# Three settings of the value phase: which sums keep a bank of their own, which bank comes first, and where the gather steps stand

## The chip, the cores and the metric

The kernel runs on one core of a Trainium2 chip. The metric is the device time of one execution in microseconds (us); lower is better. A core has TensorE (matmuls, called PE in the profile, its weight loads PEld), VectorE (DVE), ScalarE (ACT), GpSimd (POOL, which here issues the gathers of rows) and SyncE (SP, which issues the other loads). They run side by side, each through its own queue in order, and wait for one another by semaphores. Matmuls write into PSUM, which has eight banks of 128 x 512 f32 here.

## What is computed

One decoder layer: a mixer (recurrence and short convolution), then PEER, a retrieval of single-neuron experts, and a final norm. The change lies in PEER, cut here to what matters:

```python
q = (xb @ w_query).reshape(T, PEER_HEADS, 2, PEER_HALF)
s = jnp.einsum('thpk,hpnk->thpn', q, sub_keys)
...                                   # top 16 of each half, top 16 of their pairs: idx, gate
u = expert_u[idx]                     # 8 heads x 16 experts of 16384, 1024 wide
v = expert_v[idx]
act = jax.nn.gelu(jnp.einsum('td,thkd->thk', xb, u), approximate=False)
return jnp.einsum('thk,thkd->td', gate * act, v)
```

## The kernel before

The 1024 tokens are treated in two ways. For the last 672 (TD) the product with the experts is dense: all 16384 experts are taken in 128 blocks of 128 (NK = 128), every activation is computed, and a gate matrix that is zero for the experts not chosen is multiplied in. For the first 352 tokens the chosen rows of u and v are gathered from memory one expert a step, and VectorE does the sums ("gather steps"). These steps are a generator, `background()`, which the code of the dense part advances as it goes, so that both run side by side.

Every f32 operand of a matmul is split in a high part (ACT, L115) and a rest (VectorE, L116), and a product takes three matmuls: high x high, high x rest, rest x high.

The last stage (L1345 to the end) loops over the 128 blocks. For a block it does

- `u_steps`: the product of h2 with the block of u. The 672 tokens are two halves of 384 and 288 columns (SPL); each half has 24 matmuls (L1163) into one of two banks named `pa`, and ACT takes its GELU (L1168) into a tile `Wl`. Forty of the blocks (EARLIES, every third from 1 to 118) were computed in earlier stages and are loaded instead (L1450, `ged`);
- `w_step`: VectorE multiplies the gates in (L1384), then the split into `Wh` and `Wl`;
- `v_load`: the block of v is loaded and split into `vh` and `vl`.

After every third block comes a value phase (`v_phase`) of the three blocks before: 16 sums, one for each of the two halves (j = 0: 384 columns, j = 1: 288) and eight chunks of 128 outputs (c), in the order (0, 0) to (0, 7), (1, 0) to (1, 7). Each is nine matmuls (L1403). Four of the sums (FIXED) have a PSUM bank `pacc` of their own that keeps accumulating through all phases and is read once at the end. The twelve others take banks in turn from `new_pv`, alternately one of the two `pa` that the u blocks use too and one of two named `pv`; VectorE adds each into a sum in SBUF (`acc`, L1419), which frees the bank. Two and two and four banks are all eight.

A gather step is a row fetch issued on POOL (L1084, 128 rows of 4 KB) into one of five row buffers (four named `grow`, and `more` for every fifth), and one VectorE instruction on 128 x 1024: L1102 with a row of u, L1094 with a row of v. `advance(cost)` adds to an amount due and emits steps until the amount spent reaches it. In this stage `along(columns)` calls it, after every k of `u_steps` with the columns of three matmuls (L1455 to L1457), and after every sum of a value phase but the last phase's. So the steps are spread by the columns of TensorE's work (L1372 to L1377).

A scheduler then sets the order of each engine's queue from this program; the order below is its output.

Of the kernel before, what the change touches and what calls it, by code (L numbers as in the profile page):

```python
# [30 lines left out]
NK = 128  # L31
# [19 lines left out]
EARLY = 40  # L51
# [2 lines left out]
ROWS = 4  # L54
TB = 8
NE = 3.6
NF = 2.1 * TG / 64
MID = 1
WL = 3
# [2 lines left out]
WB = 2  # L62
WJ = 0
PAIRS = [(0, 2), (2, 4)]
FIXED = [(0, 1), (0, 5), (1, 1), (1, 5)]
RB = 0.15
RD = 0.0
DG = 2
# [31 lines left out]
def build(tc, A, out, dbg=None):  # L100
# [17 lines left out]
    def raw_tile(pl, shape, name, lb):  # L118

        return pl.tile(shape, F32R, name=name + "l", bufs=lb).bitcast(F32)  # L120
# [21 lines left out]
    with root:  # L142
# [29 lines left out]
        def advance(cost):  # L172
            if bg["back"] is None:
                return
            bg["due"] += cost
            while bg["spent"] < bg["due"]:
                bg["spent"] += next(bg["back"], 1e9)
# [826 lines left out]
        def norm_store(pl, o, w, parts, fw, r, sq):  # L1004

            sf = pl.tile([P, 4], F32, name="sf", bufs=3)[:w]
            for j in range(2):
                C.activation(sq[:w], parts[j], AF.Square, accum_out=sf[:, j:j + 1])
            V.scalar_tensor_tensor(sf[:, 0:1], sf[:, 0:1], DM * EPS, sf[:, 1:2], op0=OP.add, op1=OP.add)
            rsqrt(sf[:, 2:3], sf[:, 0:1], sf[:, 3:4], 5)  # L1010
            for j in range(2):
                sl = slice(j * 512, j * 512 + 512)
                V.scalar_tensor_tensor(r[:w, sl], parts[j], sf[:, 2:3], fw[:w, sl], op0=OP.mult, op1=OP.mult)
            SY.dma_start(out[o:o + w], r[:w])
# [140 lines left out]
        def u_steps(b, ge):  # L1155

            uh, ul = stationary("uT", b)
            for o, n in SPL:
                pa = psU.tile([P, 512], F32, name="pa", bufs=2)
                i = 0  # L1160
                for k in range(KC):
                    for l, r in ((uh, "h"), (uh, "l"), (ul, "h")):
                        T.matmul(pa[:, :n], l[:, k], h2[k, r][:, o:o + n], start=(i == 0), stop=(i == 3 * KC - 1))  # L1163
                        i += 1
                    if k == MID:
                        ahead()
                    if k == KC - 1:
                        C.activation(ge[:, o:o + n], pa[:, :n], AF.Gelu)  # L1168
                    yield 3.0 * n
# [10 lines left out]
        def u_early(blocks, rate):  # L1180

            left = blocks * 3.0 * KC * TD
            while left > 0:
                c = next(early, None)
                if c is None:
                    return False
                left -= c
                advance(c / 2400.0 * RATES[rate])
            return True
# [33 lines left out]
        def early_along(steps_):  # L1223
            for c in steps_:
                fill[0] += c * NE / 26.0
                if fill[0] - fill[1] > 0.25:
# [16 lines left out]
        for g in range(FULL, NG):  # L1243
            o, w = GG[g]
            r = slice(P - REST + o, P - REST + o + w)
            n = steps[g]
# [42 lines left out]
        def gates(t):  # L1289
# [3 lines left out]
            for q4 in range(w // TG):  # L1293
# [17 lines left out]
                for qb in range(TG // TB):  # L1311
# [24 lines left out]
                    advance(TB * 0.107 * RATES["F"])  # L1336
                    u_early(NF * TB / TG, "F")
                SY.dma_start(gd[:, :, (t * P) // TG + q4].rearrange("g p b t -> p g b t"),
# [4 lines left out]
        while u_early(1.0, "G"):  # L1343
# [7 lines left out]
        accs = {(j, c): mp.tile([P, n], F32, name=f"acc{j}{c}") for j, (_, n) in enumerate(SPL) for c in range(KC)  # L1351
                if (j, c) not in FIXED}
        fixed = {f: psM.tile([P, 512], F32, name=f"pacc{f[0]}{f[1]}", bufs=1) for f in FIXED}

        turn = [0]

        def new_pv():

            turn[0] ^= 1
            if turn[0]:  # L1360
                return psU.tile([P, 512], F32, name="pa", bufs=2)
            return psM.tile([P, 512], F32, name="pv", bufs=2)
# [8 lines left out]
        def along(columns):  # L1371
            advance(columns * per_column)  # L1372
# [5 lines left out]
        def g_load(q):  # L1378
            gs[q] = mp.tile([P, NTG, GB, TG], F32, name="gsb", bufs=2)
            SY.dma_start(gs[q], gd[q])  # L1380

        def w_step(b, ge):
            gv = ge.rearrange("p (n t) -> p n t", t=TG)
            V.tensor_tensor(gv, gv, gs[b // GB][:, :, b % GB], op=OP.mult)  # L1384
            Ws[b] = halves_of(mp, ge, [P, TD], "W", WS, SLOTS)

        def v_load(b):
            raw = raw_tile(mp, [P, DM], "v", VS)
            SY.dma_start(raw, A["v"][b * P:(b + 1) * P])
            Vs[b] = halves_of(mp, raw, [P, DM], "v", VS, SLOTS)  # L1390

        def v_phase(b0, b1):
            last = b1 == NK
            for j, (o, n) in enumerate(SPL):
                for c in range(KC):
                    fx = (j, c) in fixed
                    pv = fixed[j, c] if fx else new_pv()
                    i = 0
                    for b in range(b0, b1):
                        wh, wl = Ws[b]  # L1400
                        vh, vl = Vs[b]
                        for l, r in ((vh, wh), (vl, wh), (vh, wl)):
                            T.matmul(pv[:, :n], l[:, c * P:(c + 1) * P], r[:, o:o + n],  # L1403
                                     start=(i == 0 and (not fx or b0 == 0)),
                                     stop=(i == 3 * (b1 - b0) - 1 and (not fx or last)))
                            i += 1
                    if last and fx:
                        accs[j, c] = raw_tile(mp, [P, TD], "W", WS)[:, :n]
                    a = accs.get((j, c))
                    if last and fx:  # L1410
                        C.activation(a, pv[:, :n], AF.Copy, scale=modc[:, 5, c:c + 1])
                    elif last:
                        V.scalar_tensor_tensor(a, pv[:, :n], modc[:, 5, c:c + 1], a, op0=OP.mult, op1=OP.add)
                    elif fx:
                        pass
                    elif b0 == 0:
                        V.tensor_copy(a, pv[:, :n])
                    else:
                        V.tensor_tensor(a, a, pv[:, :n], op=OP.add)  # L1419
                    if not last:  # L1420
                        along(3.0 * (b1 - b0) * n)
                if last:
                    for t in range(o // P, -(-(o + n) // P)):
                        w = WT[t]
                        parts = []
                        for q in range(2):
                            pt = new_pv()[:w]
                            for c in range(4):
                                cs_ = slice((q * 4 + c) * P, (q * 4 + c + 1) * P)
                                d = pt[:, c * P:(c + 1) * P]  # L1430
                                if j:
                                    T.matmul(d, ident[:w, :w], x1s[t][:w, cs_], start=True, stop=False)
                                    T.matmul(d, accs[j, q * 4 + c][:, t * P - o:t * P - o + w], ident, start=False, stop=True)
                                else:
                                    T.transpose(d, accs[j, q * 4 + c][:, t * P - o:t * P - o + w], ident)
                            if j == 0:
                                sl = slice(q * 512, (q + 1) * 512)
                                V.tensor_tensor(rs[t][:w, sl], pt, x1s[t][:w, sl], op=OP.add)
                                pt = rs[t][:w, sl]
                            parts.append(pt)  # L1440
                        norm_store(mp, REST + t * P, w, parts, fw, rs[t], sq)
# [3 lines left out]
        for b in range(NK):  # L1445
            if b % GB == 0 and b + GB < NK:
                g_load(b // GB + 1)
            if b in EARLIES:
                ge = raw_tile(mp, [P, TD], "W", WS)
                SY.dma_start(ge, ged[EARLIES.index(b)])  # L1450
            else:
                ge = raw_tile(mp, [P, TD], "W", WS)
                for c in u_steps(b, ge):
                    along(c)
            w_step(b, ge)  # L1455
            v_load(b)
            if b - prev == SB:  # L1457
                v_phase(prev, prev + SB)
                prev += SB
        for _ in bg["back"] or ():  # L1460
            pass
        while NK - prev > SB:
            v_phase(prev, prev + SB)
            prev += SB
# [5 lines left out]
        for t in range(DT):  # L1470
            n = ("wl", "wh")[t % 2] if t < 5 else "vl"
# [69 lines left out]
```

## Time and profile before

| what | value |
|---|---|
| time, three runs | 2999.6 us median (2998.8 to 3002.2) |
| the profiled execution | 2986.6 us, its span 2984.8 us |
| PE busy | 2850.0 us, 95% of the span |
| DVE busy | 2547.3 us, 85% |
| ACT, POOL busy | 939.3 us (31%), 862.6 us (29%) |
| moved by DMA | 740 MB, 248 GB/s over the span |
| granted TensorE clock, mean | 0.981 of full |

Busy time is summed over stages with different limits, so the last stage is read by itself: it goes from the first matmul of a value phase at 1265 us to the end. There three rows of the profile are high at once, PE, DVE and DMA. "A <- B" in a wait means that engine A stood idle until B was done; the page infers it from the semaphores. A matmul's own duration there is its way through the array; what it costs is the distance from its start to the next one's start.

### The profile page before, as it was taken

Reading aid. Unit: us, or ns where it says so; the run is one execution under the profiler, and the core shown is the slowest. Engines: PE = TensorE matmul, PEld = TensorE weight load, DVE = VectorE, ACT = ScalarE, POOL = GpSimd, SP = SyncE. Lnnn points to the kernel's source line nnn. Section 1 sums busy time; section 2 is a strip of 40 time slices with the busy share of each in tenths; the row PEclk is TensorE's granted clock in tenths of the full one; section 3 lists DMA queues with packets and bytes.
Section 4 is the critical chain, followed back from the end, with each engine's and each line's share of the span. In section 5 each row is a group of like instructions: output and inputs, shape, how many; then the busy total and the mean of one; then the engine's idle time right before and its main releaser. Section 6 shows DMA issues by size and latency. Waiting matters only on the chain.

```text
span 2984.8 us, 47174 instructions
## 1 busy us (share of the span) xinstructions
PE 2850.0 (95%) x18190; PEld 2687.0 (90%) x18190; DVE 2547.3 (85%) x5369; ACT 939.3 (31%) x1548; POOL 862.6 (29%) x726
## 2 busy tenths in 40 slices
PE   8999999989999999999999999999899999899998
PEld 6887898878999889999999999999899999899998
DVE  6885549988999987488999989889899988899998
ACT  5643645333222455422222222222222222222222
POOL 0000000000000000045554544445454554555451
PEclk9999999989999999999999999999999999999999
DMA  7424342244223687788889989899899998899995
GB/s 271 146 90 140 127 155 64 78 141 146 70 90 112 212 253 244 246 307 323 324 324 330 340 321 340 325 323 332 304 351 327 329 324 316 311 327 329 324 320 182
DMA packets 288676, 740.01 MB, mean 248 GB/s; under 512 B 27873, under 2 KB 122081, under 8 KB 282050
## 3 DMA queue, kind: packets, MB, share of 16 engines
q0 software_dynamic: 102944, 374.78, 35.3%
q1 hardware_dynamic: 185506, 362.22, 35.3%
q8 instruction: 142, 2.33, 0.3%
q14 instruction: 84, 0.69, 0.1%
HBM read 666.29 MB, written 70.52 MB: 247 GB/s over the span
## 4 chain that ended last, share of the span: by engine, by line
issue 27%; DVE 25%; DMA 20%; PE 20%; POOL 5%; ACT 2%; SPq 0%; DVEq 0%; POOLq 0%; ACTq 0%
PE pp L469 5%; DVE gacc L1094 5%; DMA wl<-in_uT 3%; DVE wl L116 3%; DVE acc L1419 3%; DMA Wl<-ged 2%; PE pq L875 2%; PE pp L875 2%; DVE vl L116 2%; DVE Wl L1384 1%; DMA more<-in_u,idx 1%; PE pa L1163 1%; PE ps L579 1%; PE pp L380 1%; POOL more L1084 1%
## 5 line engine op out<-in xcount | busy, mean ns | idle before, releaser
L1163 PE MATMUL pa<-h2h,wh 128*128 128x384 f32 (+1 forms) x1840 | 590.3, 321 | 14.2 <-DVE acc L1419 12.0
L1163 PE MATMUL pa<-h2l,wh 128*128 128x384 f32 (+1 forms) x1840 | 588.0, 320 | 0.0
L1163 PE MATMUL pa<-h2h,wl 128*128 128x384 f32 (+1 forms) x1840 | 584.0, 317 | 2.7 <-DVE wl L116 2.7
L1163 PEld LDWEIGHTS pa<-h2h,wh 128*128 128x128 f32 x1840 | 347.9, 189 | 19.4 <-DVE acc L1419 13.3
L1163 PEld LDWEIGHTS pa<-h2h,wl 128*128 128x128 f32 x1840 | 349.0, 190 | 2.9 <-DVE wl L116 2.9
L1163 PEld LDWEIGHTS pa<-h2l,wh 128*128 128x128 f32 x1840 | 349.7, 190 | 0.0
L115 ACT ACTIVATE Wh<-Wl 128x672 fp32r<-128x672 f32 x128 | 98.0, 766 | 754.4 <-PE pv L1403 487.9
L115 ACT ACTIVATE wh<-wl 128x1024 fp32r<-128x1024 f32 x187 | 197.7, 1057 | 385.6 <-DMA wl<-in_uT 187.1
L1403 PE MATMUL pa<-Wh,vh 128*128 128x384 f32 (+1 forms) x768 | 251.5, 327 | 53.6 <-ACT Wl L1168 41.7
L116 DVE TENSOR_TENSOR wl<-wl,wh 128x1024 fp32r<-128x1024 f32 x187 | 228.0, 1219 | 75.3 <-ACT wh L115 74.6
L1403 PE MATMUL pv<-Wh,vh 128*128 128x384 f32 (+1 forms) x768 | 245.4, 320 | 5.2 <-DVE acc L1419 4.9
L1403 PE MATMUL pa<-Wl,vh 128*128 128x384 f32 (+1 forms) x768 | 245.8, 320 | 0.7 <-DVE Wl L116 0.7
L1403 PE MATMUL pa<-Wh,vl 128*128 128x384 f32 (+1 forms) x768 | 245.6, 320 | 0.0
L1403 PE MATMUL pv<-Wh,vl 128*128 128x384 f32 (+1 forms) x768 | 243.7, 317 | 0.0
L1403 PE MATMUL pv<-Wl,vh 128*128 128x384 f32 (+1 forms) x768 | 243.3, 317 | 0.0
L1403 PEld LDWEIGHTS pa<-Wh,vh 128*128 128x128 f32 x768 | 145.7, 190 | 67.7 <-ACT Wl L1168 52.1
L115 ACT ACTIVATE vh<-vl 128x1024 fp32r<-128x1024 f32 x128 | 134.4, 1050 | 125.5 <-DMA vl<-in_v 75.5
L1403 PE MATMUL pacc<-Wh,vh 128*128 128x384 f32 (+1 forms) x512 | 163.6, 320 | 1.5 <-ACT vh L115 1.5
L1403 PE MATMUL pacc<-Wh,vl 128*128 128x384 f32 (+1 forms) x512 | 163.7, 320 | 0.6 <-DVE vl L116 0.6
L1403 PE MATMUL pacc<-Wl,vh 128*128 128x384 f32 (+1 forms) x512 | 163.0, 318 | 0.0
L116 DVE TENSOR_TENSOR vl<-vl,vh 128x1024 fp32r<-128x1024 f32 x128 | 155.7, 1217 | 3.2 <-ACT vh L115 3.2
L469 PE MATMUL pp<-h1h,wh 128*128 128x512 f32 x384 | 157.3, 410 | 0.0
(1944 smaller groups left out, 7405.8 us busy)
## 6 DMA issues: line engine op xcount, KB each, us to landing
wl<-in_uT SPq DMA_DIRECT2D x128, 512.0 KB, 5.9
vl<-in_v SPq DMA_DIRECT2D x128, 512.0 KB, 7.9
gd<-stg SPq DMA_DIRECT2D x21, 2048.0 KB, 9.3
gsb<-gd SPq DMA_DIRECT2D x32, 1344.0 KB, 9.1
wl<-in_win SPq DMA_DIRECT2D x48, 512.0 KB, 3.5
wa<-in_wada SPq DMA_DIRECT2D x16, 1024.0 KB, 5.0
wl<-in_wq SPq DMA_DIRECT2D x32, 512.0 KB, 3.5
ged<-ge SPq DMA_DIRECT2D x40, 336.0 KB, 3.1
```

The lines of the kernel that those rows point to most:

```text
L115: C.activation(hi, src, AF.Copy)
L116: V.tensor_tensor(lo, src, hi.bitcast(F32), op=OP.subtract)
L380: T.matmul(pvs[t], l[:, t * P:(t + 1) * P], r, start=(k == 0 and l is h1[0][k] and r is wi[0]), stop=(k == KC - 1 and l is h1[1][k]))
L469: T.matmul(pp, l[:, k], r[k], start=(i == 0), stop=(i == 3 * KC - 1))
L579: T.matmul(ps_[:, c], X[:, cs_], Y[:, cs_], start=True, stop=True)
L875: T.matmul(pq[:, :m], l[:, k], hs[k, r][:, o:o + m], start=(i == 0), stop=(i == 3 * KC - 1))
L1084: G.indirect_dma_start(out=r, out_offset=None, in_=src, in_offset=IndirectOffsetOnAxis(ap=idx[:n, s0 + j:s0 + j + 1], axis=0))
L1094: V.scalar_tensor_tensor(ac, r, aw[:, j:j + 1], ac, op0=OP.mult, op1=OP.add))
L1163: T.matmul(pa[:, :n], l[:, k], h2[k, r][:, o:o + n], start=(i == 0), stop=(i == 3 * KC - 1))
L1384: V.tensor_tensor(gv, gv, gs[b // GB][:, :, b % GB], op=OP.mult)
L1403: T.matmul(pv[:, :n], l[:, c * P:(c + 1) * P], r[:, o:o + n], start=(i == 0 and (not fx or b0 == 0)), stop=(i == 3 * (b1 - b0) - 1 and (no ...
L1419: V.tensor_tensor(a, a, pv[:, :n], op=OP.add)
```

## The change

Three settings are changed. The four sums with a bank of their own become the first two, (0, 0) and (0, 1), and the last two, (1, 6) and (1, 7), where they were (0, 1), (0, 5), (1, 1) and (1, 5). The turn starts at 1, so the first bank that `new_pv` gives out is a `pv` and not a `pa`; twelve are taken in a phase, so each phase begins alike. And the columns of the u blocks count half (AU) for the gather steps, those of the value phases 1 + 0.5 x 88/128 = 1.34 (AV), so that the total stays the same.

```diff
 NE = 3.6
+
+AU = 0.5
+AV = 1.0 + (1.0 - AU) * (NK - EARLY) / NK
 NF = 2.1 * TG / 64
...
-FIXED = [(0, 1), (0, 5), (1, 1), (1, 5)]
+FIXED = [(0, 0), (0, 1), (1, 6), (1, 7)]
...
-        turn = [0]
+        turn = [1]
 
         def new_pv():
...
                     if not last:
-                        along(3.0 * (b1 - b0) * n)
+                        along(AV * 3.0 * (b1 - b0) * n)
...
                 for c in u_steps(b, ge):
-                    along(c)
+                    along(AU * c)
```

The lines move by three: L1163 becomes L1166, L1419 becomes L1422 and so on.

VectorE, before, around the start of a value phase in the later part of the loop (the phase at 2460 us of the trace): L1384 is the gate multiply, L1094 a gather step, L116 a rest of a split, L1419 the add of a bank.

```order
L1094 SCALAR_TENSOR_TENSOR gacc_19214<-grow__24606,aw_19215,gacc_19214 128x1024
L1384 TENSOR_TENSOR Wl_24538<-Wl_24538,gsb_24152 128x672
L116 TENSOR_TENSOR wl_24629<-wl_24553,wh_24628 128x1024
L116 TENSOR_TENSOR Wl_24611<-Wl_24538,Wh_24610 128x672
L1094 SCALAR_TENSOR_TENSOR gacc_19214<-more_24640,aw_19215,gacc_19214 128x1024
L116 TENSOR_TENSOR vl_24696<-vl_24693,vh_24695 128x1024
L1094 SCALAR_TENSOR_TENSOR gacc_19214<-grow__24656,aw_19215,gacc_19214 128x1024
L1094 SCALAR_TENSOR_TENSOR gacc_19214<-grow__24678,aw_19215,gacc_19214 128x1024
L1384 TENSOR_TENSOR Wl_24620<-Wl_24620,gsb_24152 128x672
L1419 TENSOR_TENSOR acc00_13115<-acc00_13115,pa_24699 128x384
L1094 SCALAR_TENSOR_TENSOR gacc_19214<-grow__24710,aw_19215,gacc_19214 128x1024
L116 TENSOR_TENSOR Wl_24690<-Wl_24620,Wh_24689 128x672
```

The same stretch now, from the gate multiply of the same u block on; the names of the lines are three higher.

```order
L1387 TENSOR_TENSOR Wl_24544<-Wl_24544,gsb_24155 128x672
L119 TENSOR_TENSOR wl_24629<-wl_24556,wh_24628 128x1024
L119 TENSOR_TENSOR Wl_24608<-Wl_24544,Wh_24607 128x672
L119 TENSOR_TENSOR vl_24614<-vl_24611,vh_24613 128x1024
L1097 SCALAR_TENSOR_TENSOR gacc_19227<-grow__24622,aw_19228,gacc_19227 128x1024
L1097 SCALAR_TENSOR_TENSOR gacc_19227<-more_24657,aw_19228,gacc_19227 128x1024
L1387 TENSOR_TENSOR Wl_24617<-Wl_24617,gsb_24155 128x672
L119 TENSOR_TENSOR vl_24690<-vl_24687,vh_24689 128x1024
L119 TENSOR_TENSOR Wl_24684<-Wl_24617,Wh_24683 128x672
L1097 SCALAR_TENSOR_TENSOR gacc_19227<-grow__24702,aw_19228,gacc_19227 128x1024
L1422 TENSOR_TENSOR acc02_13115<-acc02_13115,pv_24717 128x384
L1097 SCALAR_TENSOR_TENSOR gacc_19227<-grow__24714,aw_19228,gacc_19227 128x1024
```

Before, three gather steps stood between the rest of the last split and the gate multiply of the phase's own u block (`Wl_24620`), that multiply was the last thing ahead of the first add, and its split came after the first add. Now two steps stand there, the multiply and the split (`Wl_24617`, `Wl_24684`) are both done ahead of the first add, and the first add is that of (0, 2) from a `pv` where it was that of (0, 0) from a `pa`.

VectorE, before, at the end of a value phase earlier in the loop, from the add of (1, 0) on, with steps on rows of u (L1102) and of v (L1094):

```order
L1419 TENSOR_TENSOR acc10_13121<-acc10_13121,pa_22555 128x288
L1094 SCALAR_TENSOR_TENSOR gacc_19214<-grow__22575,aw_19215,gacc_19214 128x1024
L1419 TENSOR_TENSOR acc12_13122<-acc12_13122,pv_22578 128x288
L116 TENSOR_TENSOR wl_22675<-wl_22383,wh_22674 128x1024
L1419 TENSOR_TENSOR acc13_13123<-acc13_13123,pa_22589 128x288
L1102 SCALAR_TENSOR_TENSOR grow__22600,aw_19215<-grow__22600,hx_19212 128x1024
L1419 TENSOR_TENSOR acc14_13124<-acc14_13124,pv_22603 128x288
L1094 SCALAR_TENSOR_TENSOR gacc_19214<-grow__22623,aw_19215,gacc_19214 128x1024
L1419 TENSOR_TENSOR acc16_13125<-acc16_13125,pa_22626 128x288
L1094 SCALAR_TENSOR_TENSOR gacc_19214<-grow__22683,aw_19215,gacc_19214 128x1024
L1419 TENSOR_TENSOR acc17_13126<-acc17_13126,pv_22637 128x288
L1102 SCALAR_TENSOR_TENSOR more_22648,aw_19215<-more_22648,hx_19212 128x1024
```

The end of that phase now, from the add of (0, 7) on:

```order
L1422 TENSOR_TENSOR acc07_13120<-acc07_13120,pa_22538 128x384
L1097 SCALAR_TENSOR_TENSOR gacc_19227<-more_22549,aw_19228,gacc_19227 128x1024
L1422 TENSOR_TENSOR acc10_13121<-acc10_13121,pv_22552 128x288
L1105 SCALAR_TENSOR_TENSOR grow__22563,aw_19228<-grow__22563,hx_19225 128x1024
L1422 TENSOR_TENSOR acc11_13122<-acc11_13122,pa_22566 128x288
L1422 TENSOR_TENSOR acc12_13123<-acc12_13123,pv_22577 128x288
L1097 SCALAR_TENSOR_TENSOR gacc_19227<-grow__22588,aw_19228,gacc_19227 128x1024
L1422 TENSOR_TENSOR acc13_13124<-acc13_13124,pa_22591 128x288
L1105 SCALAR_TENSOR_TENSOR grow__22602,aw_19228<-grow__22602,hx_19225 128x1024
L1422 TENSOR_TENSOR acc14_13125<-acc14_13125,pv_22605 128x288
L1097 SCALAR_TENSOR_TENSOR gacc_19227<-grow__22616,aw_19228,gacc_19227 128x1024
L1422 TENSOR_TENSOR acc15_13126<-acc15_13126,pa_22619 128x288
```

Before, the last add of a phase was that of (1, 7), its last sum, and a split for the next u block stood among the adds. Now the last add is that of (1, 5), two sums ahead of the phase's end, and only gather steps stand among the adds.

## Rows read from the trace of the kernel before

**Rows 1.** By stretch: PE, PEld, DVE, ACT, POOL busy (count), PEclk, DMA share, GB/s.

```profile
1410.00:2767.00 1357.00, 1289.55 (x8161) 1271.24 (x8161) 1214.41 (x1672) 303.36 (x426) 692.19 (x574) 0.99 0.91 327
2810.40:2825.20 14.80, 14.80 (x98) 14.80 (x97) 14.10 (x22) 6.10 (x9) 9.56 (x8) 1.00 0.94 335
2825.20:2847.40 22.20, 22.20 (x147) 22.20 (x146) 19.84 (x34) 2.75 (x4) 13.27 (x12) 1.00 0.96 356
1540.00:1560.00 20.00, 20.00 (x122) 19.77 (x121) 18.09 (x25) 6.63 (x9) 10.86 (x9) 1.00 0.99 390
```

**Rows 2.** Waits of weight loads, 1410 to 2767: total us, times, longest.

```profile
PEld pa L1403 <- ACT Wl L1168: 47.7, 37, 3.2
PEld pa L1403 <- DVE acc L1419: 14.5, 12, 2.6
PEld pa L1163 <- DVE acc L1419: 13.3, 4, 6.4
PEld pv L1403 <- DVE acc L1419: 7.5, 12, 1.7
```

**Rows 3.** Timeline at a phase start: start, us, engine, line; idle before in brackets.

```profile
2457.15 0.85 DVE L1384 TENSOR_TENSOR Wl<-Wl,gsb 128x672 f32<-128x672 f32 x1
2458.04 0.76 ACT L115 ACTIVATE Wh<-Wl 128x672 fp32r<-128x672 f32 x1 [5.13 <-DVE Wl L1384]
2459.65 0.47 ACT L1168 ACTIVATE Wl<-pa 128x384 f32<-128x384 f32 x1
2460.18 0.45 PE L1403 MATMUL pa<-Wh,vh 128*128 128x384 f32 x1 [1.99 <-ACT Wl L1168]
```

**Rows 4.** VectorE groups, 1410 to 2767: busy us, mean ns, idle before.

```profile
L1384 DVE TENSOR_TENSOR Wl<-Wl,gsb 128x672 f32<-128x672 f32 x102 | 87.0, 853 | 34.8 <-ACT Wl L1168 17.4 <-DMA Wl<-ged 17.2
L1094 DVE SCALAR_TENSOR_TENSOR gacc<-more,aw,gacc 128x1024 f32<-128x1024 f32 x60 | 76.7, 1278 | 4.3 <-DMA more<-in_v,idx 4.0
L1102 DVE SCALAR_TENSOR_TENSOR more<-more,hx 128x1024 f32<-128x1024 f32 x54 | 65.9, 1220 | 12.3 <-DMA more<-in_u,idx 12.3
L1419 DVE TENSOR_TENSOR acc<-acc,pa 128x288 f32<-128x288 f32 x102 | 45.4, 445 | 0.4 <-PE pa L1403 0.4
```

**Rows 5.** Timeline of TensorE: first matmuls of two sums, and a seventh.

```profile
2158.92 0.33 PE L1403 MATMUL pv<-Wh,vh 128*128 128x384 f32 x1
2160.50 0.29 PE L1403 MATMUL pa<-Wh,vh 128*128 128x288 f32 x1
2161.28 0.30 PE L1403 MATMUL pa<-Wh,vh 128*128 128x288 f32 x1
```

**Rows 6.** Timeline of one late row: its issue, its step, TensorE behind it.

```profile
2121.93 0.94 POOL L1084 DMA_INDIRECT more<-in_u,idx  x1 [0.63 <-DVE gacc L1094]
2133.08 1.23 DVE L1102 SCALAR_TENSOR_TENSOR more<-more,hx 128x1024 f32<-128x1024 f32 x1 [6.29 <-DMA more<-in_u,idx]
2134.73 0.61 PE L1163 MATMUL pa<-h2h,wh 128*128 128x288 f32 x1 [6.08 <-DVE acc L1419]
```

**Rows 7.** Timeline of VectorE: steps with one add between, 384 then 288 columns.

```profile
2560.02 1.22 DVE L1102 SCALAR_TENSOR_TENSOR grow__25549<-grow__25549,hx 128x1024 f32<-128x1024 f32 x1
2561.63 1.22 DVE L1102 SCALAR_TENSOR_TENSOR grow__25563<-grow__25563,hx 128x1024 f32<-128x1024 f32 x1
2887.77 1.28 DVE L1094 SCALAR_TENSOR_TENSOR gacc<-more,aw,gacc 128x1024 f32<-128x1024 f32 x1
2889.33 1.28 DVE L1094 SCALAR_TENSOR_TENSOR gacc<-grow__28702,aw,gacc 128x1024 f32<-128x1024 f32 x1
```

**Rows 8.** DMA issues, 1410 to 2767: count, KB, median us to landing.

```profile
vl<-in_v SPq DMA_DIRECT2D x102, 512.0 KB, 7.9
more<-in_v,idx POOLq DMA_INDIRECT x61, 7.2
more<-in_u,idx POOLq DMA_INDIRECT x54, 6.7
```

**Rows 9.** Waits of ACT, 1410 to 2767: total us, times, longest.

```profile
ACT wh L115 <- DMA wl<-in_uT: 116.7, 31, 5.7
```

## Prediction

> **What bounds the kernel now.** I read the trace in this order: the busy time by stretch, the waits of TensorE, the timeline around one such wait, VectorE's groups with the idle time before them, and the DMA issues.
>
> The change acts only on the last stage (dense product, values, gather steps). I take 1410 to 2767 us of it: 34 periods, each two u blocks and one value phase, so 1357/34 = 39.9 us a period [rows 1]. Late in the run stand a pair of u blocks and a phase that nothing delayed: 14.8 and 22.2 us [rows 1]. TensorE's floor is thus 37.0 us a period, 34 x 37.0 = 1258 us, and 1357 - 1258 = 99 us lie above it.
>
> The waits account for that 99. The weight loads, which stand before the matmuls and show a whole stall, waited 47.7 us for ACT at L1168 with a value phase next, 14.5 + 7.5 us for VectorE's adds within a phase, and 13.3 us for such an add before a u block [rows 2]: 83.0 us. The granted clock was 0.99 of full in this stretch [rows 1]; the missing hundredth is 14 us. Together they are 97 of the 99.
>
> The timeline shows where the largest comes from. ACT had nothing to do for 5.13 us because the gate multiply of a finished u block (L1384) started only at 2457.15, behind gather steps in VectorE's queue. The split Wh that waits for it, and the next GELU behind that in ACT's queue, came late: that GELU started at 2459.65, and the first sum of the phase, which wants the bank it reads, at 2460.18, 1.99 us late [rows 3]. So a late VectorE reaches TensorE through ACT and through the bank that the phase takes first.
>
> VectorE is itself nearly full: 1214.4 us busy of 1357, that is 35.7 us a period, and 4.2 idle [rows 1]. Of this idle time the buffer "more", every fifth gathered row, shows 4.0 + 12.3 us of waiting for its row [rows 4]; five times that, some 82 us (an estimate), goes to rows of all buffers. Another 34.8 us stands before the gate multiply, half of it for a late GELU [rows 4].
>
> **The change, part by part.**
>
> *Fixed sums first, and rotation from pv.* A sum of nine matmuls at 384 columns takes 2160.50 - 2158.92 = 1.58 us; at 288 columns one matmul comes each (2161.28 - 2160.50)/6 = 0.13 us, a sum 1.17 [rows 5]. Before, the first sum takes one pa bank at once and the second pa bank comes at matmul 28, 3 x 1.58 = 4.74 us in. Now two fixed sums and one in pv stand ahead, so the first pa bank is wanted 4.74 us in and the second, after five sums, 7.9 us in. The longest wait for L1168 was 3.2 us [rows 2], below the 4.74 added at the first place and equal to the 3.16 added at the second. Where both came in one phase, a remainder is left. Of 47.7 us I take 46 as gone, and with these waits nearly all the half-speed matmuls after them: 9 of the 14 us. From below: were GELU later still, half would stay (-24); from above, -47.7 and all of the 14.
>
> *Half the steps beside u.* The gather total is the same: 88 u blocks at 0.5 and 128 blocks of values at 1.34 weigh 216, as 88 + 128 did. Counted in the order, seven or eight steps now stand between the last add of a phase and the first of the next, and about ten between its first and last add, both much as before. What moved out from between the adds is the gate multiply and the splits (two or three a phase). They now stand ahead of the first add, where the u stretch has fewer steps, so ACT is fed earlier. That supports the 46 above; I give it no term of its own.
>
> *Fixed sums last.* The last two sums have no add, so VectorE gets 2 x 1.17 = 2.3 us after its last evacuation before a u block wants a bank. The 13.3 us came in four waits, one of 6.4 us [rows 2], caused by a row: issued at 2121.93, its step started at 2133.08, with an add behind it and a u block behind that [rows 6]. Cover of 2.3 us does not remove such a wait, and takes the small ones: -7. Bounds: 0 and -13.3.
>
> *Twelve rotating sums in a row.* This is the cost. From the end of the first rotating sum to the end of the twelfth TensorE needs 5 x 1.58 + 6 x 1.17 = 14.9 us, where it had 7 x 1.58 + 8 x 1.17 = 20.4 before. VectorE's pace of an add and a step is 2561.63 - 2560.02 = 1.61 us at 384 columns and 2889.33 - 2887.77 = 1.56 at 288 [rows 7]: ten steps and twelve adds are 5 x 1.61 + 5 x 1.56 and two adds without a step, 2 x 0.45 [rows 4], together 16.7 us. It ends 1.8 us late. TensorE may run three sums ahead, 3 x 1.17 = 3.5 us, so without row waits nothing stalls, and 1.7 us are left. With five row buffers, a row's round is landing, step and POOL's turn: 7 + 1.25 + 0.63 = 8.9 us [rows 4, 6, 8], 1.78 a row against 1.6. The first five have landed when the phase begins; the next five add 5 x 0.18 = 0.9 us, within the 1.7. Rows vary, though, and the 22 us of add waits inside a phase I put up by 8. Bounds: -22 (all gone), and +90 (3.3 us a period, as in the last rival, against the 22 of now).
>
> *The ends.* Before 1265 us nothing moves. In the tail four steps instead of two stand behind the last add: 2 x 1.28 = 2.6 us [rows 4], against two sums, 2.3 us, that VectorE need not add. I take 0, bounds -3 and +5.
>
> Sum: -46 - 9 - 7 + 8 = -54. The profiled execution took 2986.6 us (span 2984.8), so 2933 for one like it; on the median of 2999.6, 13 us above, that is 2946 us. It leaves (99 - 54)/34 = 1.3 us a period above TensorE's floor, 38.3 us, of which VectorE would be busy 35.7: its idle time has to fall from 4.2 to 2.6 us a period. That is the hardest demand of the forecast.
>
> *DMA.* 327 GB/s moved at a share of 0.91, and 20 us stand at 390 with 0.99 [rows 1]. At 38.3 us a period the same bytes need 327 x 39.9/38.3 = 341 GB/s. I charge nothing.
>
> Rows and loads of 512 KB land in much the same time, 7.2 and 6.7 us against 7.9 [rows 8]. The Trainium skill (DMA: Bandwidth & Descriptors, section Queues, rings and completion order) says that each DMA engine takes the queues it has work for in turn, packet by packet; the like landings agree with that. By it a gathered row beside one of SP's loads would get half of the 390, 2.7 us for 512 KB instead of 1.34, and denser rows in a phase would land later, which speaks against the change: the +8 would grow toward the last rival's price. No row shows by how much.
>
> **Rivals.**
> 1. *VectorE's row waits stay* (20%). If its 82 us of row waits only move from the u blocks to the phases, 2.4 us a period, and some of the waits before the gate multiply stay, a period is 35.7 + 2.4 + 1.0 = 39.1: 0.8 x 34 = 27 us gained at best, and nothing if all stay. Time 2973 to 2999; I write 2983. For it: VectorE has no other slack. Against: GELU's share of its waits is a result of its own lateness.
> 2. *TensorE's floor* (10%). Slack in the banks takes all that is left: -99, 2901 to 2915. Against: long row landings remain [rows 6].
> 3. *Banks are not the cause* (5%). If weights for the next u block bind instead (ACT waited 116.7 us for them [rows 9]), the wait goes from the phase's start to the next u block: L1168's 47.7 us return there, -54 + 47.7 = -6, 2993. Against: no u block waited for its weights in rows 2.
> 4. *Slower* (8%). Rows landing later in the dense phase. VectorE's lateness at its last add is 1.8 + (landing + 1.9 - 8.0), and TensorE stalls by what exceeds 3.5. From a landing of 7.8 us on it stalls; beyond 10.7 us the stall passes the 2.9 us that a period has above its floor now, and the kernel is slower. At 11.1, the long landing of [rows 6], it is 3.3 us: +0.4 x 34 = 14 us, 3014. It needs most rows that late, where the medians are 7.2 and 6.7.
>
> **How the numbers follow.** The forecast, -25 to -80 us, holds 57%: 2946, its own range 2920 to 2975. Its low end and rival 2 join at 2912. The upper end takes in rivals 1 and 3 to 2996. About 0.2% (6 us) is what a measurement here can tell from no change. Faster by more: the forecast's 57, rival 2's 10 and 15 of rivals 1 and 3, 82%. Within: 9%. Slower: rival 4 and a little of the tail, 9%.
>
> **What would show it.** Right: waits of a phase's first matmuls for L1168 under 5 us in total; a granted clock at 1.00; u stretches near 14.8 to 15.2 us; VectorE's idle time near 90 us over the same periods, with the waits for rows now inside the phases. Wrong: waits for L1419 inside phases well above 30 us would mean that the dense steps bind (rivals 1 and 4); waits at a u block's first matmuls, rival 3. The forecast fails if VectorE's idle time stays at 4 us a period.

## The result and the profile after

The changed kernel took 3015.65 us (median, 3006.19 to 3020.45) against 2998.75 (2985.80 to 3004.61) of the kernel before on the same chip: a ratio of 1.0060, 95% interval 1.0044 to 1.0077. It is slower by some 17 us; forecast were 2946 us, 54 us faster. The profiled execution of before, which the prediction starts from, was with 2986.6 us among its quickest, so differences between traces come out smaller than those between medians.

Busy time of the changed kernel in the stretch of [rows 1], with the same columns:

```profile
1410.00:2767.00 1357.00, 1295.67 (x8095) 1260.22 (x8093) 1204.85 (x1663) 307.09 (x425) 725.42 (x571) 0.99 0.90 325
```

VectorE did less work in the same time, 1204.85 us for 1214.41, 1663 instructions for 1672. It sat idle for 1357 - 1204.85 = 152.2 us where it was 142.6: the idle time that had to fall rose. The granted clock stayed at 0.99.

Waits of the weight loads of the changed kernel (total us, times, longest), which answer to [rows 2]:

```profile
PEld pv L1406 <- DVE acc L1422: 31.8, 44, 2.3
PEld pa L1406 <- DVE acc L1422: 28.9, 46, 3.8
PEld pa L1166 <- ACT Wl L1171: 10.5, 15, 2.2
PEld pa L1166 <- DVE wl L119: 8.9, 13, 1.4
PEld pacc L1406 <- ACT vh L118: 7.2, 2, 5.6
...
PEld pa L1166 <- DVE acc L1422: 0.5, 1, 0.5
```

The 47.7 us of a phase for the GELU are gone, as forecast: no row has L1406 waiting for L1171. The 13.3 us before a u block are 0.5. But the adds inside a phase hold TensorE for 31.8 + 28.9 = 60.7 us, where it was 14.5 + 7.5 = 22.0, and u blocks wait for weights (the split `wl`), which they did not.

VectorE's groups of the changed kernel (busy us, mean ns, idle before it and its releaser) say what VectorE waited for:

```profile
L119 DVE TENSOR_TENSOR vl<-vl,vh 128x1024 fp32r<-128x1024 f32 x102 | 124.2, 1218 | 18.7 <-ACT vh L118 18.7
...
L1387 DVE TENSOR_TENSOR Wl<-Wl,gsb 128x672 f32<-128x672 f32 x102 | 86.9, 852 | 10.5 <-ACT Wl L1171 10.5
...
L119 DVE TENSOR_TENSOR wl<-wl,wh 128x1024 fp32r<-128x1024 f32 x68 | 83.0, 1220 | 65.7 <-ACT wh L118 65.5
L1097 DVE SCALAR_TENSOR_TENSOR gacc<-more,aw,gacc 128x1024 f32<-128x1024 f32 x59 | 75.5, 1279 | 1.8 <-DMA more<-in_v,idx 1.2 <-DVE acc L1422 0.4
L1105 DVE SCALAR_TENSOR_TENSOR more<-more,hx 128x1024 f32<-128x1024 f32 x55 | 67.2, 1221 | 2.4 <-DMA more<-in_u,idx 2.3
```

The gate multiply's wait fell from 34.8 to 10.5 us and the rows' of "more" from 4.0 + 12.3 to 1.2 + 2.3 [rows 4]. Rows hold VectorE less: over all five buffers its waits for rows sum up to 44 us, where it was 89. In their place stands the rest of the split of the next uT block, `wl`: 65.5 us of waiting for ACT's `wh`. The group of before had 9.6:

```profile
L116 DVE TENSOR_TENSOR wl<-wl,wh 128x1024 fp32r<-128x1024 f32 x68 | 83.0, 1220 | 9.7 <-ACT wh L115 9.6
```

And ACT's `wh` waits for the load of the block. One such place in the timeline of the changed kernel (start, us, engine, line; idle before in brackets):

```profile
1820.14 0.33 SPq L206 DMA_DIRECT2D wl<-in_uT  x1
...
1824.31 0.86 DVE L119 TENSOR_TENSOR Wl<-Wl,Wh 128x672 fp32r<-128x672 f32 x1 [0.83 <-ACT Wh L118]
...
1825.36 0.47 PE L1166 MATMUL pa<-h2h,wl 128*128 128x384 f32 x2
...
1829.59 1.06 ACT L118 ACTIVATE wh<-wl 128x1024 fp32r<-128x1024 f32 x1 [5.31 <-DMA wl<-in_uT]
1830.55 0.47 ACT L1171 ACTIVATE Wl<-pa 128x384 f32<-128x384 f32 x1
1830.68 1.23 DVE L119 TENSOR_TENSOR wl<-wl,wh 128x1024 fp32r<-128x1024 f32 x1 [5.50 <-ACT wh L118]
1833.45 1.06 ACT L118 ACTIVATE vh<-vl 128x1024 fp32r<-128x1024 f32 x1 [2.43 <-DMA vl<-in_v]
1834.54 1.23 DVE L119 TENSOR_TENSOR vl<-vl,vh 128x1024 fp32r<-128x1024 f32 x1 [2.64 <-ACT vh L118]
1834.56 0.69 PE L1406 MATMUL pacc<-Wh,vh 128*128 128x384 f32 x1 [5.26 <-ACT vh L118]
```

The load was issued at 1820.14 and landed about 1829.5. ACT stood at its copy for 5.31 us, with a GELU behind it in its queue whose last matmuls had started by 1825.36. VectorE stood 5.50 us at the rest of the same split, with the rest of `vl`, a gate multiply and all adds of the next phase behind it. TensorE's 5.26 us in this place ended with something else, the copy of a block of v that had not landed before 1833.45. (The Trainium skill, Perfetto Trace Analysis, section Tensor Engine Instruction (MATMUL, LD_WEIGHTS), says that ACT and VectorE are strictly first in, first out; the trace agrees: the GELU stands 5 us behind a copy it has nothing to do with.)

Both loads were issued right behind a load of gates (`gsb`) of 1344 KB in SP's queue:

```profile
1817.31 0.32 SPq L1383 DMA_DIRECT2D gsb<-gd  x1
...
1820.52 0.50 SPq L1392 DMA_DIRECT2D vl<-in_v  x1
```

That is no single case. Of the seven waits of VectorE for `wh` that passed 4 us, six came 12.4 to 13.4 us after the issue of such a load; they are 29 of the 65.5 us.

So what does TensorE pay? Its weight loads wait 93.9 us in all, where it was 84.9: 60.7 for adds in the phases, 19.9 at the u blocks (GELU 10.5, weights 8.9, an add 0.5), and 13.3 at the first sums of a phase (`pacc`).

ACT's waits for uT are not new ([rows 9]: 116.7 us, 31 times; now):

```profile
ACT wh L118 <- DMA wl<-in_uT: 135.1, 48, 6.1
```

What is new is that VectorE waits along. Letters for VectorE's instructions, from its order in one steady period of each kernel (M gate multiply, W v u the rests of the splits of W, v and uT, g gather step, a add), show it:

```
before               W vgg v MgWuggg MvW agagagagM agagagaua...
fixed sums, AU 1     W vgggvuMgWgggvMgW agaMuagagagaagagaagaagg
whole change, AU .5  gg MvWuggMvWugMvWgg agagagagagagagagagaagagg
```

At half the rate both u of a period stand right behind a W, ahead of the first add; before, one stood among the adds or had steps ahead of it. Of the 81 such splits in the loop, 5 stood right behind a W and ahead of the adds in the kernel before, and 41 do now; 24 stood among the adds, and 2 do now. Pairing each load's issue with the start of ACT's copy gives a median of 9.8 us between them before (31 of 68 under 8 us) and 6.1 us in the changed kernel (50 of 68 under 8). In the median the loads do not land later: those that ACT waited for took 5.8 us from issue to copy before and 5.9 now. But 12 of these 48 were issued within 6 us behind a load of gates and took 8.4 us, the others 5.7; before it was 4 of 31.

### The profile page after: what moved, and what is told of

The parts are those of the page before. It is cut to its first block, busy times and chain, and to the rows that moved or that the text cites. A ratio compares the mean times of both kernels' runs of the same rounds, so it can differ in the third digit from the quotient of the medians.

```text
span 3012.5 us, 47082 instructions
## 1 busy us (share of the span) xinstructions
PE 2872.9 (95%) x18190; PEld 2688.6 (89%) x18190; DVE 2544.8 (84%) x5369; ACT 943.6 (31%) x1548; POOL 900.1 (30%) x726
## 4 chain that ended last, share of the span: by engine, by line
PE 35%; DVE 30%; DMA 19%; issue 9%; POOL 3%; ACT 3%; SPq 0%; DVEq 0%; POOLq 0%; ACTq 0%
PE pa L1166 12%; DMA wl<-in_uT 7%; PE pp L472 5%; DVE gacc L1097 4%; PE pa L1406 3%; DVE wl L119 3%; PE pv L1406 3%; PE pacc L1406 3%; DMA vl<-in_v 2%; DVE acc L1422 2%; PE pg L1333 2%; PE pp L878 2%; DVE s L929 1%; DVE vl L119 1%; ACT wh L118 1%
## 5 line engine op out<-in xcount | busy, mean ns | idle before, releaser
L1166 PE MATMUL pa<-h2h,wh 128*128 128x384 f32 (+1 forms) x1840 | 590.4, 321 | 10.4 <-ACT Wl L1171 7.0
L1166 PE MATMUL pa<-h2h,wl 128*128 128x384 f32 (+1 forms) x1840 | 583.2, 318 | 8.1 <-DVE wl L119 7.7
L1166 PE MATMUL pa<-h2l,wh 128*128 128x384 f32 (+1 forms) x1840 | 587.4, 319 | 0.0
L1166 PEld LDWEIGHTS pa<-h2h,wh 128*128 128x128 f32 x1840 | 347.3, 189 | 17.6 <-ACT Wl L1171 11.4
L1166 PEld LDWEIGHTS pa<-h2h,wl 128*128 128x128 f32 x1840 | 348.4, 189 | 12.3 <-DVE wl L119 12.3
L1166 PEld LDWEIGHTS pa<-h2l,wh 128*128 128x128 f32 x1840 | 348.7, 190 | 0.0
L1406 PE MATMUL pv<-Wh,vh 128*128 128x384 f32 (+1 forms) x768 | 251.0, 327 | 28.5 <-DVE acc L1422 27.1
L1406 PE MATMUL pa<-Wh,vh 128*128 128x384 f32 (+1 forms) x768 | 252.4, 329 | 20.2 <-DVE acc L1422 18.2
L1406 PE MATMUL pa<-Wh,vl 128*128 128x384 f32 (+1 forms) x768 | 245.2, 319 | 0.0
L1406 PE MATMUL pa<-Wl,vh 128*128 128x384 f32 (+1 forms) x768 | 244.6, 319 | 0.0
L1406 PE MATMUL pv<-Wh,vl 128*128 128x384 f32 (+1 forms) x768 | 244.2, 318 | 0.0
L1406 PE MATMUL pv<-Wl,vh 128*128 128x384 f32 (+1 forms) x768 | 243.9, 318 | 0.0
L1406 PEld LDWEIGHTS pv<-Wh,vh 128*128 128x128 f32 x768 | 145.6, 190 | 43.8 <-DVE acc L1422 42.1
L1406 PEld LDWEIGHTS pa<-Wh,vh 128*128 128x128 f32 x768 | 146.2, 190 | 36.0 <-DVE acc L1422 33.6
L1406 PE MATMUL pacc<-Wh,vh 128*128 128x384 f32 (+1 forms) x512 | 164.2, 322 | 11.8 <-ACT vh L118 9.8
L1406 PE MATMUL pacc<-Wh,vl 128*128 128x384 f32 (+1 forms) x512 | 164.6, 322 | 2.8 <-DVE vl L119 2.8
L1406 PE MATMUL pacc<-Wl,vh 128*128 128x384 f32 (+1 forms) x512 | 163.4, 320 | 1.5 <-DVE Wl L119 1.5
```

## The experiments

Theory A: VectorE, in order, stands at the split of a uT block whose load was issued some 6 us earlier, since few steps now stand beside the u blocks. Its rivals: B, twelve rotating sums in a row are too dense; C, the loads land late because rows crowd them out; D, the thin stretch beside u costs by itself, whatever the loads do. Each ratio is to the kernel before on the same chip, with its 95% interval.

**Fixed sums alone, without and with rotation from pv** (AU = 1 in both; the first keeps `turn = [0]`)

```diff
-FIXED = [(0, 1), (0, 5), (1, 1), (1, 5)]
+FIXED = [(0, 0), (0, 1), (1, 6), (1, 7)]
-        turn = [0]
+        turn = [1]     # second kernel only
```

> The fixed sums at both ends alone, first bank pa, steps spread as before. Theory A (VectorE's queue reaches the splits of loads that have not landed, because few steps stand beside u): no loss, 2975 to 3000 us, VectorE's waits for the split of weights near the 10 us of before. Theory B (twelve rotating sums in a row are too dense for VectorE's adds): slower, 3010 to 3020 us, waits of TensorE for adds within phases near 60 us as after the whole change.

> Fixed sums at both ends and rotation from pv, steps spread as before. Theory A: faster than before, 2960 to 2990 us, since the waits for GELU at a phase's start (47.7 us) go and no load stands at the head of VectorE's queue. Theory B: slower, 3010 to 3020 us, waits for adds within phases near 60 us.

Measured: 2961.72 us, 0.9861 (0.9837 to 0.9884), and 2964.44 us, 0.9863 (0.9839 to 0.9886). Waits of the weight loads and the group of `wl` in the second:

```profile
PEld pv L1406 <- DVE acc L1422: 34.4, 41, 3.9
PEld pa L1406 <- DVE acc L1422: 16.5, 31, 2.2
PEld pacc L1406 <- DVE Wl L119: 7.4, 8, 2.0
```

```profile
L119 DVE TENSOR_TENSOR wl<-wl,wh 128x1024 fp32r<-128x1024 f32 x70 | 85.3, 1219 | 6.6 <-ACT wh L118 6.3 <-issue 0.2
```

The twelve dense sums with 50.9 us of add waits inside the phases are there, and the kernel is 41 us faster: B falls. The first kernel came out below the 2975 to 3000 us that A had for it. The rotation's first bank makes no difference.

Against the whole change, the waits of the weight loads are 68.0 us in all for 93.9: 10 us less for adds, 18 less at the u blocks (1.7 for 19.9), 4.5 less at the first sums, and one wait of 6.3 us elsewhere that the whole change has not. So it is at the u blocks that TensorE pays most for the rates, and the adds wait long in both.

**The rates alone**

```diff
-AU = 1.0
+AU = 0.5
```

> The rates alone (half the steps beside u), fixed sums and first bank as before. Theory A: slower than before, 3005 to 3025 us, VectorE waits over 50 us for the weights' split by ACT. Theory B: within 8 us of before, 2992 to 3005 us, waits for adds within phases near the 22 us of before.

Measured: 3038.09 us, 1.0122 (1.0097 to 1.0148), above the 3005 to 3025 us of A.

```profile
L119 DVE TENSOR_TENSOR wl<-wl,wh 128x1024 fp32r<-128x1024 f32 x65 | 79.2, 1218 | 56.3 <-ACT wh L118 55.4 <-PE pa L1166 0.8
```

```profile
PEld pa L1166 <- ACT Wl L1171: 34.7, 26, 2.9
PEld pa L1166 <- DVE wl L119: 25.3, 24, 2.2
```

The wait for `wh` comes with the rates, under the old fixed sums too, and there TensorE's u blocks pay for it. The edit that I gave no term costs 37 us by itself, and 59 beside the fixed sums (1.0060 against 0.9863).

**The whole change at 0.75, and at 0.6**

```diff
-AU = 0.5
+AU = 0.75     # 0.6 in the second kernel
```

> The whole change with AU at 0.75 in place of 0.5. Theory A: between the fixed sums with pv first and the whole change, 2985 to 3008 us, VectorE's waits for the weights' split 20 to 45 us. Theory B: like the whole change, 3010 to 3020 us.

> The whole change with a rate of 0.6 instead of 0.5 beside u (and 1.28 instead of 1.34 beside the values). In VectorE's order the second split of a period then stands at the first add again, as at 0.75, and not between the two gate multiplies as at 0.5. Theory A by place: the time is that of 0.75, 0.982 to 0.990 of the kernel before. Theory D (a cost that grows with the number of steps taken from the u blocks): at 0.75 it cost nothing and at 0.5 some 50 us, so 0.6 lies between, 0.993 to 1.002.

Measured: 0.75, 2957.31 us, 0.9841 (0.9819 to 0.9862), the lowest of the complete kernels, though not clear of the fixed sums alone; 0.6, 2973.96 us, 0.9920 (0.9894 to 0.9946). The groups of `wl` and `vl` at 0.75, then at 0.6, and the add waits at 0.75:

```profile
L119 DVE TENSOR_TENSOR vl<-vl,vh 128x1024 fp32r<-128x1024 f32 x105 | 127.8, 1217 | 8.6 <-ACT vh L118 8.6
...
L119 DVE TENSOR_TENSOR wl<-wl,wh 128x1024 fp32r<-128x1024 f32 x70 | 85.3, 1218 | 8.9 <-ACT wh L118 8.9
```

```profile
L119 DVE TENSOR_TENSOR vl<-vl,vh 128x1024 fp32r<-128x1024 f32 x105 | 127.9, 1218 | 32.7 <-ACT vh L118 32.6
...
L119 DVE TENSOR_TENSOR wl<-wl,wh 128x1024 fp32r<-128x1024 f32 x69 | 84.0, 1218 | 11.2 <-ACT wh L118 11.2
```

```profile
PEld pv L1406 <- DVE acc L1422: 30.2, 39, 2.9
PEld pa L1406 <- DVE acc L1422: 24.8, 37, 4.9
```

At 0.75 A as first put, with a cost that grows with the thinning (2985 to 3008 us, 20 to 45 us of waiting), failed, and B with it; hence the second form of A, by the place of the split. Counted in VectorE's order as above, 10 of the 81 splits of uT stand right behind a W at 0.75 and 13 at 0.6 (7 with the fixed sums alone), and the wait stays near 10 us; at 0.5 it is 41 splits and 65.5 us, with the rates alone 47 and 55.4. The time does not keep to A's figure for 0.6, though: 0.992 lies above 0.982 to 0.990 and just under D's 0.993 to 1.002. The split of the next block of v, thinned out likewise, waits 32.6 us there, but that does not explain it: VectorE's idle time in the stretch is 119.0 us at 0.6 and 120.2 at 0.75, and the weight loads wait 63.5 and 67.8 us in all. Of the 14.1 us between the two profiled spans, 9.0 lie ahead of the first matmul of a value phase (1270.4 and 1261.4 us), where the rates do not act yet. That the thinning itself makes 0.6 costlier than 0.75 is thus not shown; the jump to 0.5 is.

**The split of uT half a block later**

```diff
-                    if k == MID:
+                    if k == MID and o:
                         ahead()
```

> The whole change, with the split of the next uT block written half a block later (behind the second column part's first products instead of the first part's), which moves it behind one or two more gather steps in VectorE's queue in most periods, the loads as they were. Theory A by place: each step or so of delay hides 1.3 to 2.6 of the 2 to 5 us that such a wait lasts; ACT's waits for uT fall by a third to a half and the time to 0.990 to 1.002 of the kernel before, unless the split then comes too late for the next u block. Theory C (the loads land late because the rows crowd them out): the load lands with the split, so the wait at the split shrinks but TensorE's stalls do not; 1.003 to 1.009.

Measured: 2991.96 us, 0.9973 (0.9957 to 0.9989), 0.9% below the changed kernel. VectorE waited 52.2 us for `wh`, 13 less, and 19 splits stand right behind a W. A part comes back by place, within A's range; C expected no gain. The waits fell by less than A had it: VectorE's by a fifth, ACT's own for uT only from 135.1 to 127.1 us, where a third to a half was expected. VectorE's waits for rows fell as well, from 44 to 28 us, and its wait for `vh` rose from 18.7 to 34.2, so the gain is not that of the split of uT alone.

**Loads with buffers of their own**

```diff
         mp = pool(stM, "mp")
+        deepen(mp, len(order) - NK + len(EARLIES), NK - len(EARLIES), 3)
-WS = SLOTS + 2
+WS = SLOTS + 1
```

> The whole change, and in the last stage every third block of uT has a buffer pair of its own and the next weights are prepared up to two blocks ahead; in exchange one buffer of the gate blocks W less. VectorE's order stays almost that of the changed kernel; only the loads are issued earlier. Theory A (VectorE stands at the split of a uT block whose load was issued only some 6 us before): most of the waits of ACT's split for uT go (65 us of VectorE's idle time in 1410 to 2767 us of the changed kernel to under 25), and the time falls by 25 to 55 us from the changed kernel's, to 0.982 to 0.995 of the kernel before. Theory D (what costs is the thin stretch beside u and the dense adds themselves, whatever the loads do): the time stays within 8 us of the changed kernel's, 1.003 to 1.009 of before.

Measured: 3028.00 us, 1.0094 (1.0071 to 1.0117).

```profile
L119 DVE TENSOR_TENSOR wl<-wl,wh 128x1024 fp32r<-128x1024 f32 x44 | 53.7, 1220 | 50.3 <-ACT wh L118 47.3 <-PE pv L1407 3.1
L119 DVE TENSOR_TENSOR wxl<-wl,wxh 128x1024 fp32r<-128x1024 f32 x22 | 26.8, 1219 | 17.3 <-ACT wxh L118 17.2
```

A miss of the edit: it moved the splits forward as far as the loads, so that ACT's copy still came 6.3 us behind the issue (median) and VectorE still waited 47.3 + 17.2 = 64.5 us; and it took a buffer away. With the wait, the time did not fall either, which agrees with A, but it tells A from D no better than before.

**No loads of uT in the last stage, in the changed kernel and in the fixed sums alone**

```diff
-                SY.dma_start(raws[n], A[src][i])
+                if n < len(order) - NK + len(EARLIES):
+                    SY.dma_start(raws[n], A[src][i])
...
+                        split(hi, lo, h2[0, "h"].bitcast(F32)[:, None, :P].to_broadcast([P, KC, P]))
```

> The whole change, and in the last stage the blocks of uT are not loaded: their split takes columns of a tile already there (this leaves out those loads, so the first product there is not the reference's). The split instructions keep their number and length. VectorE's order moves a little with it, in some periods the second split stands one place later. About 34 of the 441 MB in 1410 to 2767 us are not moved. Theory A (VectorE stands at the splits for uT): the time is that of the fixed sums alone without these loads (the next run), within 12 us, and both at 0.970 to 0.984 of the kernel before. Theory D (the thin stretch beside u costs by itself): it stays 30 us or more above the next run.

> Fixed sums at both ends and rotation from pv with the full rate beside u, and the blocks of uT not loaded in the last stage (left out as in the run before). VectorE's order is that of the same kernel with the loads. VectorE waited little for uT there (about 10 us), so theories A and D both expect a small gain over its 0.9863: 0.974 to 0.986 of the kernel before, from the 8 per cent of traffic that are gone.

Measured: 2923.24 us, 0.9768 (0.9751 to 0.9785), and 2933.03 us, 0.9789 (0.9776 to 0.9801). Waits of the weight loads in the first:

```profile
PEld pa L1413 <- DVE acc L1429: 18.6, 36, 4.7
PEld pv L1413 <- DVE acc L1429: 12.3, 27, 1.9
```

With the loads the change at 0.5 was 2.0% behind the fixed sums alone; without them it is level or a little ahead. The 59 us thus go with the loads of uT: A holds, D falls. That the rows gain from the lighter traffic is not what the pair shows: VectorE's waits for rows fell by 11 us in the first kernel (44 to 33) and not at all in the second (72 and 73). The add waits inside the phases fell from 60.7 to 30.9 us, but from 50.9 to 30.0 in the second kernel too, where the split had hardly been late; they do not mark the late split. (VectorE's order moved with the edit, 25 splits of 81 stand right behind a W and no longer 41, so the pair shows loads and place together, not the place alone.)

**No row fetches**

```diff
-                    G.indirect_dma_start(out=r, out_offset=None, in_=src,
-                                         in_offset=IndirectOffsetOnAxis(ap=idx[:n, s0 + j:s0 + j + 1], axis=0))
```

> The whole change with no gathered row fetched (the gather steps take a row already there; this leaves out the fetches, and the steps' results are not the reference's). VectorE's instructions are the same in number and length. Theories A and C: the loads have the DMA engines nearly to themselves and land in about 3.5 us instead of 6, so the waits for uT at VectorE's queue fall below 15 us in 1410 to 2767 us, the row waits go too, and the time comes to 2890 to 2930 (0.965 to 0.977). Theory D: the dense adds still stall TensorE inside the phases, 40 us or more of add waits, and the time stays above 2960 (0.987).

Measured: 2882.37 us, 0.9618 (0.9592 to 0.9643). The stretch, and the issues of uT (count, KB, median us to landing):

```profile
1410.00:2767.00 1357.00, 1355.19 (x8752) 1346.69 (x8751) 1293.80 (x1811) 332.81 (x460) 0.00 (x0) 1.00 0.33 114
```

```profile
wl<-in_uT SPq DMA_DIRECT2D x74, 512.0 KB, 3.5
```

```profile
L119 DVE TENSOR_TENSOR wl<-wl,wh 128x1024 fp32r<-128x1024 f32 x74 | 90.3, 1220 | 32.7 <-ACT wh L118 32.1
```

TensorE is busy for 1355.19 of 1357 us, and its weight loads wait 10.1 us in all: about its floor. VectorE's order stayed nearly the same (37 splits of 81 right behind a W), and at 0.5 neither it nor its density costs TensorE much once loads land in 3.5 us, which goes against B and D. The time came out 8 us below the range of A and C, though VectorE's wait for `wh` did not fall below 15 us: 32.1 us of it stayed, in 26 short waits of at most 2.4 us, and TensorE had no use for that time. A uT load lands in 3.5 us; with the rows beside it (the kernel with the split half a block later) in 6.1. This run does not part A from C.

**The two halves of the fixed sums** (AU = 1, rotation from pv)

```diff
-FIXED = [(0, 0), (0, 1), (1, 6), (1, 7)]
+FIXED = [(0, 0), (0, 1), (1, 1), (1, 5)]     # first kernel
+FIXED = [(0, 1), (0, 5), (1, 6), (1, 7)]     # second kernel
```

> Of the fixed sums only the two at the start of a phase (with rotation from pv), in the second column part the old places; the full rate beside u. The forecast's terms -46 and -9 belong to this part and -7 to the other. Of the 41 us that both gave together this part then gives 35 to 41: 0.986 to 0.989 of the kernel before. Rival: the two sums at the end, which give VectorE 2.3 us before the next u block, do half of it; then 0.991 to 0.995.

> Of the fixed sums only the two at the end of a phase, in the first column part the old places; rotation from pv, the full rate beside u. By the forecast's terms -7: 0.995 to 1.000 of the kernel before. With rotation from pv the first sum of a phase takes a pv bank, so the first wait for the GELU moves by one sum, 1.58 us, which may add some 10 to 20 us of gain. Rival: this part does half of the whole, 0.991 to 0.995.

Measured: 2983.85 us, 0.9961 (0.9948 to 0.9975), and 2982.05 us, 0.9948 (0.9930 to 0.9967). Waits of the weight loads of the first, then of the second:

```profile
PEld pa L1166 <- DVE acc L1422: 48.2, 31, 6.4
PEld pv L1406 <- DVE acc L1422: 21.8, 21, 2.4
PEld pa L1406 <- DVE acc L1422: 7.7, 8, 2.1
```

```profile
PEld pv L1406 <- DVE acc L1422: 34.9, 29, 6.0
PEld pa L1406 <- DVE acc L1422: 14.5, 27, 2.9
PEld pv L1406 <- DVE Wl L119: 11.0, 10, 2.0
PEld pa L1406 <- ACT Wl L1171: 3.0, 3, 1.3
```

In both the 47.7 us for the GELU are all but gone, and each is only 12 to 16 us faster. With the first sums alone the stall moved to the next u block, which waits 48.2 us for an add where it was 13.3. With the last sums alone it moved to the adds inside. Together they give 41, more than 12 + 16: my split of the gain into -46 - 9 for the start and -7 for the end was wrong, and so was my expectation for the first; the second lies between the two forecast for it.

## Why the prediction was wrong

One account holds all runs: VectorE's idle time in 1410 to 2767 us (1357 less its busy time in the row of that stretch) against the ratio.

| kernel | VectorE idle, us | ratio |
|---|---|---|
| rates alone | 171.2 | 1.0122 |
| own buffers | 167.7 | 1.0094 |
| whole change | 152.2 | 1.0060 |
| before | 142.6 | 1 |
| first sums alone | 134.8 | 0.9961 |
| last sums alone | 133.3 | 0.9948 |
| split half a block later | 128.4 | 0.9973 |
| AU 0.75; 0.6 | 120.2; 119.0 | 0.9841; 0.9920 |
| fixed sums; with rotation from pv | 113.9; 119.2 | 0.9861; 0.9863 |
| whole change; fixed sums, no uT loads | 88.8; 97.2 | 0.9768; 0.9789 |
| no row fetches | 63.2 | 0.9618 |

A line through these 14 points rises by 0.00046 a us (correlation 0.98), 1.4 us of time for one us in this stretch; the whole stage is about 1.3 times as long. It is an account and not a cause: VectorE's work is fixed, so its busy time in a stretch of fixed length tells how far the kernel has come. The total waits of TensorE's weight loads in the stretch follow the ratio as closely (0.98; from 10.1 us without rows to 111.6 with the rates alone), and ACT's busy time nearly so (-0.97), though ACT is busy for less than a quarter of it. What it does teach is that the totals count and not a single row: the 47.7 us for the GELU are all but gone in each half of the fixed sums, but TensorE's waits fell by 2 and 17 us in all.

- *Half the steps beside u.* This is the step that failed. I wrote that "ACT is fed earlier" and gave it no term; it costs 59 us beside the fixed sums. The steps and adds ahead of the split were cover: while ACT waited 116.7 us for uT [rows 9], VectorE had steps to do, and its split met a copy already made. I named ACT's wait only for rival 3, and not what hid it from VectorE. That a `wl` stood among the adds before, and only gather steps now, is in the rows of VectorE's order ahead of the prediction; I counted the steps and left out that the split moved forward toward its load. In TensorE's waits this shows at the u blocks, 19.9 us where it was 13.5, and 1.7 with the fixed sums.
- *Fixed sums first, -46 and -9.* The mechanism was right, L1168's wait is gone in every kernel with these sums. As a gain it was mis-sized: alone they gave 12 us, because the lateness was VectorE's and went to the next u block (48.2 us). The 9 for half-speed matmuls did not come either: the granted clock of the stretch stayed at 0.99 [rows 1].
- *Fixed sums last, -7.* The wait is 0.5 us, better than forecast, and without this part the first would have gained little.
- *Twelve sums in a row, +8.* Mis-sized: the add waits rose by 38.7 us in the changed kernel and by 28.9 with the fixed sums alone. But this is not what made the change slow: they are 55.0 us at 0.75 and 60.1 at 0.6, in kernels that are faster than before. The sign of being wrong that I gave, add waits well above 30 us, came true and pointed at the wrong cause.
- *Rows.* I took them for what may come late. VectorE waited less for them, 44 us for 89 (my estimate for before was 82), so rival 4 falls; that its 3014 us are within 2 us of the measured time is luck. What came late was a load by SP.
- *DMA, at no charge.* The rate was 325 GB/s, not more than before. In the median the loads did not land later than before (5.9 against 5.8 us), so the charge lay mainly in where they were waited for: C falls as the main cause by that, and by the gain from the later split. A part of it holds: more of the waited loads stood behind a load of gates (12, before 4). No run takes these apart from the place.
- *The range.* Its upper end stood on rivals 1 and 3; the only slower one rested on rows. No rival had VectorE's queue stand at a load.

The fixed sums alone, -41 us, lay in the range; the whole was 20 us above its upper end. What stays open: why the order changes so abruptly between 0.6 and 0.5, why 0.6 came out slower than 0.75, and how much of the cost belongs to the loads behind the gates.

## What to carry to other kernels

Count an edit by the total of the waits of the engines that are nearly full, not by the one row that it removes; a stall that goes may only move. Before filler work is taken from a stretch, list the waits of the other queues that it hides: each instruction behind it moves forward toward a load that lands no earlier. A wait of 117 us on an engine that costs little is a debt that becomes due when its cover goes.

## What the runs showed of the hardware

A 512 KB load by SP landed in 3.5 us where no rows were fetched and in 6.1 beside them (medians). The Trainium skill (DMA: Bandwidth & Descriptors, section Queues, rings and completion order) has each DMA engine take its queues in turn; the slower landing agrees with that. A single load of uT could take 9.4 us (1820.14 to about 1829.5 above), half again that median; it stood behind a load of 1344 KB issued 2.8 us earlier by the same engine.
